# The first sixty microseconds of a hybrid backbone: modulation products in column tiles, and a gather of unit 0 beside the loads

## The chip, the core and the metric

The kernel runs on one core of a Trainium2 chip. The core has a TensorE for matrix products (PE in the profile; its weight loads are PEld), VectorE (DVE), ScalarE (ACT), GpSimd (POOL) and SyncE (SP), whose queue here issues nearly all transfers. TensorE's clock has two levels, 1.2 and 2.4 GHz; the profile shows the granted share of the higher one. The metric is the device time of one execution in microseconds. The bytes come from HBM into SBUF, products land in PSUM.

## What is computed

One layer of a diffusion backbone over 512 latent and 256 context tokens of width 1024. What matters here is its beginning:

```python
m_l = jax.nn.silu(c) @ w_ada[i] + b_ada[i]          # six vectors of 1024 for the latent
m_c = jax.nn.silu(c_ctx) @ w_ada[i] + b_ada[i]      # and for the context
u_l = modulate(x, sh1_l, sc1_l) @ w_in[i]           # modulate: layer_norm(x) * (1 + scale) + shift
u_c = modulate(xc, sh1_c, sc1_c) @ w_in[i]
mix_c, mix_l = token_mixer(u_c, u_l, ...)           # two scans in both directions, 8 heads
x = layer_norm(ALPHA * x + g1_l * (mix_l @ w_out[i]), ...)
y_l = peer(modulate(x, sh2_l, sc2_l), ...)          # product keys, 16384 experts of one neuron
x = layer_norm(ALPHA * x + g2_l * y_l, ...)
```

The first two of the six vectors (shift 1 and scale 1) are needed before any column of `u` can be computed. The gate of four of the heads is of rank 16: 32 columns of `u`, the gate rank, are multiplied by `w_gk2` later. All is in float32; the large products are made of three products of rounded parts (`mm3`: high by high, high by low, low by high).

## The kernel before

**Stages.** `Net.mixer` does the norm and modulation of all tokens (the pools `first` and `fps`), then six units of heads, each with `project` (its columns of `u`) and `scan`, then the output projection; `Peer` does the rest, about two thirds of the time. A loop in `mixer` calls `project`, `scan` and `mods_second` (m2, the other four vectors, one step at a time) by three running sums, and a list scheduler then places the instructions on the engines' queues by their dependences. Each queue runs in order.

**The beginning, by loops.** `mods_first` goes over four groups g of 512 columns of the first two vectors. A group has four loads `wada1` of 512 KB (two k of 128 rows each), eight products `pmr` that put the two conditions (latent, context) on 2 partitions by 512 columns and sum over k in PSUM, a copy `mrow`, four transposes `pm`, and two additions into `m1`. `first_norm` goes over six blocks b of 128 tokens (four latent, then two context): load `xin`, statistics, `xn`, eight transposes `pT`, two copies into `xt`. `modulate_first` makes, for each k of 128 channels and each of latent and context, the high part `hTh` on ScalarE and the low part `hTl` by two operations (`hT`, then `hTl`) on VectorE. `NN` says how many blocks are normed ahead of each group. Groups 0 and 1 give the k 0 to 3 their shifts and scales, and so on; k 0 to 5 are modulated behind group 2 and k 6, 7 behind group 3.

**Then**, one behind the other: `gate_rank` (32 products `pr`: 64 rows out of the columns `wr`, high and low), and in `project` of unit 0 the context values (`pt`, 24 products of 256 columns, a transposition), four blocks of 128 tokens by 256 columns of values and output gate (`pt`, 96 products), and the column products `pc` of `proj_c` for the two forget gates and the query. The value weights of unit 0, `w_tf`, are split into `wh` and `wl` by `token_slabs` ahead of that. PSUM tiles of the projections come from the pool `pj`, three buffers.

**Around it.** `scan_consts` (masks, lower bounds, six small loads) is called at the end of the beginning. `mods_second` first makes `silrow`, a row of 1024 conditions on all partitions (two halves, eight passes of ScalarE, four of VectorE), and then columns: each is a load of 256 KB and one operation of VectorE with a sum. It is stepped for the first time between groups 0 and 1. A transfer waits for the landing of the eighth ahead of it in the same queue, beside what its buffer waits for.

Of the kernel before, what the change touches and what calls it, by code (L numbers as in the profile page):

```python
# [8 lines left out]
F32 = mybir.dt.float32  # L9
F32R = mybir.dt.float32r  # L10
# [19 lines left out]


NN = (1, 3, 2, 0)


class Net:
# [112 lines left out]
    def mods_first(self, pers, pool, ps):  # L148

        nc, a = self.nc, self.a  # L150
        t1 = pool.tile([128, 8, 2], F32, name="cct1")
        t2 = pool.tile([128, 8, 2], F32, name="cct2")
        sil = pool.tile([128, 8, 2], F32, name="sil")
        self.log_sigmoid(sil, self.cc, t1, t2)
        nc.scalar.activation(sil, sil, AF.Exp)
        nc.vector.tensor_tensor(sil, sil, self.cc, op=OP.mult)
# [4 lines left out]
        for g in range(4):  # L161
            ws = [pool.tile([128, 2, 512], F32, name="wada1", bufs=8) for _ in range(4)]
            for i, w in enumerate(ws):
                nc.sync.dma_start(w, a["w_ada1"][g][:, i * 2:i * 2 + 2])
            p = ps.tile([2, 512], F32, name="pmr", bufs=2)
            for k in range(8):
                nc.tensor.matmul(p, sil[:, k, :], ws[k // 2][:, k % 2, :], start=k == 0, stop=k == 7)
            mrow = pool.tile([2, 512], F32, name="mrow", bufs=2)
            nc.vector.tensor_copy(mrow, p)
            pm = ps.tile([128, 4, 2], F32, name="pm", bufs=1)  # L170
            for m in range(4):
                nc.tensor.transpose(pm[:, m, :], mrow[:, m * 128:(m + 1) * 128], self.ident[0:2, 0:2])
# [3 lines left out]
            yield  # L176
# [89 lines left out]
    def first_norm(self, pool, ps, xt):  # L266

        nc, a = self.nc, self.a
        for b in (2, 3, 4, 5, 0, 1):
            x = pool.tile([128, D], F32, name="xin", bufs=2)  # L270
            nc.sync.dma_start(x, a["ctx"][b * 128:(b + 1) * 128] if b < 2 else a["x"][(b - 2) * 128:(b - 1) * 128])
            mu, rs = self.norm_stats(pool, x, "a")
            n = pool.tile([128, D], F32, name="xn", bufs=2)
            nc.vector.tensor_scalar(n, x, mu, rs, op0=OP.subtract, op1=OP.mult)
            for g in range(2):
                p = ps.tile([128, 4, 128], F32, name="pT")
                for i in range(4):
                    k = g * 4 + i
                    nc.tensor.transpose(p[:, i, :], n[:, k * 128:(k + 1) * 128], self.ident)
                nc.scalar.activation(xt[:, g * 4:g * 4 + 4, b * 128:(b + 1) * 128], p, AF.Copy)  # L280
            yield

    def modulate_first(self, pool, xt, ks):
# [461 lines left out]
    def mixer(self, es):  # L745
# [12 lines left out]
        with tc.tile_pool(name="first", bufs=1) as fp, tc.tile_pool(name="fps", bufs=2, space=PSUM) as fps:  # L758
# [11 lines left out]
            for g in range(4):  # L770
                for _ in range(NN[g]):
                    next(norm)
# [578 lines left out]
```

## Time and profile before

| | |
|---|---|
| median of three runs | 1774.92 us (1774.51 to 1775.79) |
| profiled execution | 1771.05 us, its span 1768.9 us |
| TensorE busy | 1711.5 us (97%), 10485 products |
| VectorE busy | 1448.7 us (82%) |
| ScalarE busy | 833.1 us (47%) |
| granted TensorE clock, mean | 0.988 |

A row of a timeline gives the start in us, the busy time of the group, engine, line, operation, tiles written and read, shapes (contraction rows by columns of the weights, then the moving operand), the count, and in brackets the idle time of the engine just before with what ended it. A matmul's record lasts longer than its share of the engine, since they are pipelined: the step from start to start is what one costs. In a row of groups, the figures behind the bar are busy us in sum, and mean ns of one.

### The profile page before, as it was taken

How to read it: one execution, taken by the hardware profiler on the slowest of the kernel's cores; microseconds unless marked ns; L12 is line 12 of the kernel's file. 1: busy time of each engine (PE TensorE's matmuls, PEld its weight loads, DVE VectorE, ACT ScalarE, POOL GpSimd, SP SyncE). 2: the span in 40 equal slices, each digit the busy share in tenths (PEclk: the TensorE clock that was granted, in tenths of full speed). 3: DMA queues.
4: the chain of work that ended last, by engine and by line, in shares of the span. 5: the costliest groups of instructions: out<-in, count | busy, mean ns of one | idle time of the engine just before them, and what ended most of it. 6: DMA issues, size and time to landing. Idle time of an engine off the chain costs nothing. (4 is left out here: it accounts for less than half of the span.)

```text
span 1768.9 us, 28164 instructions
## 1 busy us (share of the span) xinstructions
PE 1711.5 (97%) x10485; PEld 1484.2 (84%) x10485; DVE 1448.7 (82%) x2913; ACT 833.1 (47%) x1417; POOL 406.4 (23%) x285
## 2 busy tenths in 40 slices
PE   6999999999989999999999999999999999999997
PEld 2788887877778999999998899999999998888886
DVE  6669879877779999999996887787778786776768
ACT  5467676665233355776674333333333333333332
POOL 0000000000023102238522544344344442111000
PEclk9999999999989999999999999999999999999999
DMA  8523525415232247988999999989989989998862
GB/s 302 176 83 130 179 82 149 135 67 203 73 104 84 72 142 273 324 323 308 333 327 355 341 360 343 318 313 336 319 311 337 314 309 314 351 340 293 266 218 96
DMA packets 174811, 428.99 MB, mean 243 GB/s; under 512 B 14993, under 2 KB 78801, under 8 KB 170578
## 3 DMA queue, kind: packets, MB, share of 16 engines
q1 hardware_dynamic: 137234, 290.87, 48.5%
q0 software_dynamic: 36864, 134.23, 21.6%
q8 instruction: 82, 1.34, 0.3%
q10 hardware_dynamic: 576, 2.10, 0.3%
q14 instruction: 55, 0.45, 0.1%
HBM read 378.38 MB, written 48.76 MB: 241 GB/s over the span
## 5 line engine op out<-in xcount | busy, mean ns | idle before, releaser
L142 PE MATMUL pH<-hh,uh 128*128 128x384 f32 x1024 | 350.1, 342 | 1.0 <-ACT gels L1081 1.0
L144 PE MATMUL pH<-hh,ul 128*128 128x384 f32 x1024 | 347.6, 340 | 1.5 <-DVE ul L1068 1.5
L143 PE MATMUL pH<-hl,uh 128*128 128x384 f32 x1024 | 347.0, 339 | 0.0
L142 PE MATMUL y<-vh,ah 128*128 128x512 f32 x768 | 302.7, 395 | 4.1 <-ACT ah L1107 4.1
L144 PE MATMUL y<-vh,al 128*128 128x512 f32 x768 | 301.9, 395 | 0.4 <-DVE al L1108 0.4
L143 PE MATMUL y<-vl,ah 128*128 128x512 f32 x768 | 301.4, 392 | 0.0
L1068 DVE TENSOR_TENSOR vl<-vr,vh 128x1024 fp32r<-128x1024 f32 x128 | 156.7, 1224 | 154.9 <-ACT vh L1066 154.8
L1137 POOL DMA_INDIRECT erow<-in_u_dram,ix x128 | 188.8, 1475 | 371.7 <-DVE scr L1146 213.8
L1137 POOL DMA_INDIRECT erow<-in_v_dram,ix x128 | 184.2, 1439 | 327.9 <-DVE yg L1154 182.5
L1066 ACT ACTIVATE vh<-vr 128x1024 fp32r<-128x1024 f32 x128 | 135.1, 1056 | 200.4 <-issue 127.8
L1107 ACT ACTIVATE ah<-gel 128x384 fp32r<-128x384 f32 x128 | 66.8, 524 | 279.8 <-DVE gel L1104 278.0
L142 PEld LDWEIGHTS pH<-hh,uh 128*128 128x128 f32 x1024 | 192.4, 188 | 3.8 <-ACT gels L1081 1.4
L143 PEld LDWEIGHTS pH<-hl,uh 128*128 128x128 f32 x1024 | 192.7, 188 | 2.7
L144 PEld LDWEIGHTS pH<-hh,ul 128*128 128x128 f32 x1024 | 192.3, 188 | 2.5 <-DVE ul L1068 2.4
L1066 ACT ACTIVATE uh<-ur 128x1024 fp32r<-128x1024 f32 x128 | 135.0, 1055 | 116.3 <-PE pH L143 67.6
L144 PEld LDWEIGHTS y<-vh,al 128*128 128x128 f32 x768 | 144.7, 188 | 35.1 <-DVE al L1108 0.8
L142 PEld LDWEIGHTS y<-vh,ah 128*128 128x128 f32 x768 | 144.5, 188 | 34.9 <-ACT ah L1107 4.7
L143 PEld LDWEIGHTS y<-vl,ah 128*128 128x128 f32 x768 | 144.5, 188 | 30.7
L1068 DVE TENSOR_TENSOR ul<-ur,uh 128x1024 fp32r<-128x1024 f32 x128 | 155.7, 1217 | 15.7 <-PE pH L144 13.6
L1154 DVE SCALAR_TENSOR_TENSOR yg<-erow,act,yg 128x1024 f32<-128x1024 f32 x127 | 162.3, 1278 | 0.1
L1146 DVE SCALAR_TENSOR_TENSOR scr<-erow,h 128x1024 bf16<-128x1024 f32 x128 | 155.9, 1218 | 0.0
L142 PE MATMUL pc<-hTh,wh 128*128 128x512 f32 (+1 forms) x304 | 109.6, 361 | 0.4 <-ACT V L398 0.4
(358 smaller groups left out, 3055.8 us busy)
## 6 DMA issues: line engine op xcount, KB each, us to landing
ur<-in_uT_dram SPq DMA_DIRECT2D x128, 512.0 KB
vr<-in_v_dram SPq DMA_DIRECT2D x128, 512.0 KB
Gd<-stage SPq DMA_DIRECT2D x24, 1024.0 KB
Gn<-Gd SPq DMA_DIRECT2D x16, 1536.0 KB
wraw<-in_w_cf_dram SPq DMA_DIRECT2D x24, 512.0 KB
wada<-in_w_ada_dram SPq DMA_DIRECT2D x48, 256.0 KB
Hd<-gels SPq DMA_DIRECT2D x56, 192.0 KB
gel<-Hd SPq DMA_DIRECT2D x56, 192.0 KB
```

What stands on the lines that cost most here:

```text
L142: mm(out, lh, rh, start=start, stop=False)
L143: mm(out, lh, rl, start=False, stop=False)
L144: mm(out, ll, rh, start=False, stop=stop)
L1066: nc.scalar.activation(hi, raw, AF.Copy)
L1068: sub = eng.tensor_tensor(lo, raw, hi, op=OP.subtract)
L1107: nc.scalar.activation(ah, g, AF.Copy)
L1137: nc.gpsimd.indirect_dma_start(out=e, out_offset=None, in_=a[src], in_offset=bass.IndirectOffsetOnAxis(ap=self.ix[:, j:j + 1], axis=0))
L1146: nc.vector.scalar_tensor_tensor(scr, e, 1.0, h2, op0=OP.mult, op1=OP.mult, accum_out=dots[:, j:j + 1])
L1154: nc.vector.scalar_tensor_tensor(y, e, act[:, j:j + 1], y, op0=OP.mult, op1=OP.add)
```

## The change

Five things are done.

- `mods_first` gives `sil` 32 columns (two conditions, the rest zero) and puts product k on partitions 32 (k mod 4) and on, so that four products stand in four column tiles of 32; each tile sums two k. The sums of the four tiles are made by four products with `sel`, a selection of the partitions 0 and 1 of each 32, which take the place of the four transposes.
- `gate_rank` and the first part of `project` of unit 0 are gone; `begin` does, for one k after another, the three products of the context values, the two of the gate rank on context and two on latent, and the twelve of the values. It is stepped by two k, between the groups. The sums stay in PSUM over all eight k: all three buffers of `pj` (now the pool of the whole mixer) and one of `fps`.
- The loads: four blocks of x, then group 0, then the small ones of `scan_consts`, the context blocks, `wr`, the value weights, and groups 1 to 3. `first_norm` is one generator for each block, four buffers, and the norm is made in place.
- k 0 and 1 are modulated behind group 0 already, two k behind each group; latent and context of the first two k apart.
- `mods_second` is stepped for the first time in the loop over the units: its `silrow` and all its columns stand behind the beginning.

```diff
@@ mods_first
-        sil = pool.tile([128, 8, 2], F32, name="sil")
+        sil = pool.tile([128, 8, 32], F32, name="sil")
+        sc = sil[:, :, 0:2]
+        nc.vector.memset(sil, 0.0)
...
         for g in range(4):
+            yield
             ws = [pool.tile([128, 2, 512], F32, name="wada1", bufs=8) for _ in range(4)]
             for i, w in enumerate(ws):
                 nc.sync.dma_start(w, a["w_ada1"][g][:, i * 2:i * 2 + 2])
-            p = ps.tile([2, 512], F32, name="pmr", bufs=2)
+            yield
+            p = ps.tile([128, 512], F32, name="pmr", bufs=1)
             for k in range(8):
-                nc.tensor.matmul(p, sil[:, k, :], ws[k // 2][:, k % 2, :], start=k == 0, stop=k == 7)
-            mrow = pool.tile([2, 512], F32, name="mrow", bufs=2)
+                j = k % 4 * 32
+                nc.tensor.matmul(p[j:j + 32, :], sil[:, k, :], ws[k // 2][:, k % 2, :], start=k < 4, stop=k > 3)
+            mrow = pool.tile([128, 512], F32, name="mrow", bufs=2)
             nc.vector.tensor_copy(mrow, p)
             pm = ps.tile([128, 4, 2], F32, name="pm", bufs=1)
             for m in range(4):
-                nc.tensor.transpose(pm[:, m, :], mrow[:, m * 128:(m + 1) * 128], self.ident[0:2, 0:2])
+                nc.tensor.matmul(pm[:, m, :], mrow[:, m * 128:(m + 1) * 128], sel, start=m == 0, stop=m == 3)
@@ project
-            ws = self.ahead.pop(u, None) or self.token_slabs(u)
-            p = self.pj.tile([128, TC], F32, name="pt", tag="pj")
-            for k in range(8):
+            begun = self.ahead.pop(u, None)
+            ws = None if begun else self.token_slabs(u)
+            p = begun[0] if begun else self.pj.tile([128, TC], F32, name="pt", tag="pj")
+            for k in range(0 if begun else 8):
@@ begin
+        for k in range(8):
+            wh, wl = (t[:, k % 4, :] for t in slabs[k // 4])
...
+            for p, sl in ((pc, slice(0, TC)), (pl, slice(TC, TA))):
                 for i, h in enumerate((self.hTh, self.hTl)):
+                    nc.tensor.matmul(p, wr[:, k, :], h[:, k, sl], start=p is pl and k + i == 0,
+                                     stop=p is pl and k + i == 8)
...
+            for b in range(2, 6):
+                sl = slice(b * 128, (b + 1) * 128)
+                self.mm3(vg[b // 2 - 1][:, b % 2, :], self.hTh[:, k, sl], self.hTl[:, k, sl], wh, wl,
+                         k == 0 and b % 2 == 0, k == 7 and b % 2 == 1)
+            if k % 2:
+                yield
@@ mixer
-            norm, mods = self.first_norm(fp, fps, xt), self.mods_first(self.c, fp, fps)
-            seq = (0, 1, 4, 2, 5, 3)
-            for g in range(4):
-                for _ in range(NN[g]):
-                    next(norm)
-                if g == 1:
-                    next(m2)
-                if g == 2:
-                    self.ahead = {seq[0]: self.token_slabs(seq[0])}
-                next(mods)
-                if g > 1:
-                    self.modulate_first(fp, xt, range(0, 6) if g == 2 else range(6, 8))
-            self.scan_consts(self.mp, fp)
...
+            step(*norm[:4], mods, mods)
+            self.scan_consts(self.mp, fp)
+            step(norm[0], norm[1], norm[4], norm[5])
...
+            begin = self.begin(seq[0], fps, slabs, wr)
+            step(norm[2], norm[3], mods, mods)
+            self.modulate_first(fp, xt, range(0, 2), lat)
+            step(norm[4], norm[5])
+            self.modulate_first(fp, xt, range(0, 2), ctx)
+            for g in (1, 2, 3):
+                step(mods, begin, mods)
+                self.modulate_first(fp, xt, range(2 * g, 2 * g + 2), lat, ctx)
+            step(begin, begin)
...
-        self.gate_rank()
```

What the scheduler makes of it is seen in the queues. On TensorE, at the end of the third group and in the fourth, there stood before (`pmr` products of the groups' loads, `pm` transposes, then `pr`, the gate rank):

```order
L167 MATMUL pmr<-wada_428,sil 2x512 x2
L172 MATMUL pm<-ident,mrow 128x2 x4
L167 MATMUL pmr<-wada_429,sil 2x512 x2
L167 MATMUL pmr<-wada_430,sil 2x512 x2
L167 MATMUL pmr<-wada_431,sil 2x512 x2
L593 MATMUL pr<-hTh,wh 64x256
L593 MATMUL pr<-hTl,wh 64x256
```

and in the new order stand, from the first product of the fourth group on (`pt` are the gather's products, also those of `wrs`, the gate rank on context; `pr` is its gate rank on latent):

```order
L178 MATMUL pmr<-wada_529,sil 32x512 x2
L178 MATMUL pmr<-wada_530,sil 32x512 x2
L178 MATMUL pmr<-wada_531,sil 32x512 x2
L139 MATMUL pt<-hTh,wh 128x256
L140 MATMUL pt<-hTl,wh 128x256
L141 MATMUL pt<-hTh,wl 128x256
L610 MATMUL pt<-hTh,wrs 64x256
L610 MATMUL pt<-hTl,wrs 64x256
L178 MATMUL pmr<-wada_532,sil 32x512 x2
L610 MATMUL pr<-hTh,wrs 64x512
L610 MATMUL pr<-hTl,wrs 64x512
L139 MATMUL pt<-wh,hTh 128x256
```

The products of the fourth group have moved between those of the gather of k 4, and the gate rank has moved from behind all of them into the gather. On SyncE the queue began with one block, group 0 and two more blocks:

```order
L760 DMA cc<-in_ccol_dram 128x16
L762 DMA wr<-in_w_r_dram 128x256
L271 DMA xin<-in_x_dram 128x1024
L159 DMA b_140<-in_b1col_dram 128x16
L164 DMA wada_143<-in_w_ada_dram 128x1024
L164 DMA wada_144<-in_w_ada_dram 128x1024
L164 DMA wada_145<-in_w_ada_dram 128x1024
L164 DMA wada_146<-in_w_ada_dram 128x1024
L271 DMA xin<-in_x_dram 128x1024 x2
```

and now has (in brackets the semaphores waited for; `lbz`, `w` and `bgk` are small loads of `scan_consts`, a DMAHW semaphore counts the landing of an earlier transfer):

```order
L280 DMA xin<-in_x_dram 128x1024 x4
L167 DMA b_130<-in_b1col_dram 128x16
L173 DMA wada_133<-in_w_ada_dram 128x1024
...
L173 DMA wada_136<-in_w_ada_dram 128x1024 [waits DMAHW1_49]
L78 DMA lbz<-in_hg_lb_dram 128x8 [waits DMAHW2_49]
L100 DMA w_192<-in_w_gk_dram 16x256 [waits DMAHW3_49,DVE_49]
...
L103 DMA bgk<-in_b_gk_dram 128x4 [waits DMAHW7_49]
L280 DMA xin<-in_ctx_dram 128x1024 [waits DMAHW0_49,DVE_49,PE_49]
L280 DMA xin<-in_ctx_dram 128x1024 [waits DMAHW1_49,DVE_49,PE_49]
L798 DMA wr<-in_w_r_dram 128x256 [waits DMAHW2_49]
```

The small loads have moved from the end of the beginning to a place between group 0 and the context blocks. On VectorE, behind the last `hTl`, there stood before the columns of m2 (`wada,m2h`), ahead of the first gate operation of unit 0:

```order
L205 SCALAR_TENSOR_TENSOR wada_1347,m2h<-wada_1347,silrow 128x512
L301 TENSOR_TENSOR wl<-wraw,wh 128x1024
L205 SCALAR_TENSOR_TENSOR wada_1350,m2h<-wada_1350,silrow 128x512
L301 TENSOR_TENSOR wl<-wraw,wh 128x1024
L205 SCALAR_TENSOR_TENSOR wada_1353,m2h<-wada_1353,silrow 128x512
L209 TENSOR_TENSOR m_242<-m2h 128x8
L115 SCALAR_TENSOR_TENSOR gs_717<-G,gs_716 128x512
L210 TENSOR_TENSOR m_242<-m_242,b2col 128x8
L329 TENSOR_TENSOR G<-G,gs_717 128x512
L205 SCALAR_TENSOR_TENSOR wada_1625,m2h<-wada_1625,silrow 128x512
```

and now, from the second half of `silrow` on, the columns stand between those of the gate (`gs`, `Z`, `LF`, up to the scan `BP`):

```order
L309 TENSOR_TENSOR wl<-wraw,wh 128x1024
L215 SCALAR_TENSOR_TENSOR wada_1100,m2h<-wada_1100,silrow 128x512
L112 SCALAR_TENSOR_TENSOR gs_757<-Z,gs_756 128x768
L215 SCALAR_TENSOR_TENSOR wada_1245,m2h<-wada_1245,silrow 128x512
L387 SCALAR_TENSOR_TENSOR Z<-gs_757,lbl_185,Z 128x768
L215 SCALAR_TENSOR_TENSOR wada_1248,m2h<-wada_1248,silrow 128x512
L391 TENSOR_SCALAR gs_757<-gs_757,lbl_185,lbA 128x768
L215 SCALAR_TENSOR_TENSOR wada_1251,m2h<-wada_1251,silrow 128x512
L392 TENSOR_TENSOR LF<-gs_757,gs_756 128x768
L215 SCALAR_TENSOR_TENSOR wada_1254,m2h<-wada_1254,silrow 128x512
L437 SCALAR_TENSOR_TENSOR BP<-rmask,LF 128x768
```

The weighted columns have moved behind the gate's first operations and the row `silrow` has come with them.

## Rows read from the trace of the kernel before

**Rows 1.** Windows: busy us (instructions) of PE, PEld, DVE, ACT, POOL; clock, DMA, GB/s.

```profile
20.00:40.00 20.00, 14.01 (x53) 4.92 (x53) 13.40 (x24) 11.96 (x23) 0.00 (x0) 0.91 0.90 337
...
60.00:80.00 20.00, 19.53 (x142) 18.37 (x142) 11.88 (x28) 6.00 (x12) 0.00 (x0) 1.00 0.69 202
80.00:100.00 20.00, 19.00 (x114) 16.68 (x113) 13.32 (x26) 13.14 (x19) 0.00 (x0) 1.00 0.48 147
```

**Rows 2.** Timeline of TensorE, 10 to 74 us.

```profile
10.96 6.17 PE L167 MATMUL pmr<-wada,sil 128*2 128x512 f32 x14
17.06 1.10 PE L279 MATMUL pT<-ident,xn 128*128 128x128 f32 x8
...
53.15 0.40 PE L172 MATMUL pm<-ident,mrow 2*128 2x2 f32 x4
...
57.55 0.39 PE L593 MATMUL pr<-hTh,wh 128*64 128x512 f32 x1
57.78 0.40 PE L593 MATMUL pr<-hTl,wh 128*64 128x512 f32 x1
...
61.83 0.36 PE L142 MATMUL pt<-wh,hTh 128*128 128x256 f32 x1
...
73.43 0.40 PE L142 MATMUL pc<-hTh,wh 128*128 128x512 f32 x1
```

**Rows 3.** Timeline of VectorE: its first statistics of a block.

```profile
5.36 1.29 DVE L122 BATCH_NORM_STATS2 sta<-xin 128x6 f32<-128x512 f32 x2 [0.75 <-DMA xin<-in_x_dram]
```

**Rows 4.** VectorE by groups, shapes apart, the first 75 us.

```profile
L205 DVE SCALAR_TENSOR_TENSOR wada<-wada,silrow 128x512 f32<-128x512 f32 x13 | 8.8, 690 | 7.3 <-DMA wada<-in_w_ada_dram 7.2
L122 DVE BATCH_NORM_STATS2 sta<-xin 128x6 f32<-128x512 f32 x12 | 7.8, 681 | 2.3 <-DMA xin<-in_x_dram 2.2
L291 DVE TENSOR_TENSOR hTl<-hT,hTh 128x512 fp32r<-128x512 f32 x8 | 5.4, 673 | 0.0
L274 DVE TENSOR_SCALAR xn<-xin,mva,rsa 128x1024 f32<-128x1024 f32 x6 | 4.8, 806 | 0.6 <-ACT rsa L131 0.6
L290 DVE TENSOR_SCALAR hT<-xt,m 128x512 f32<-128x512 f32 x8 | 4.3, 541 | 0.9 <-ACT xt L280 0.9
L301 DVE TENSOR_TENSOR wl<-wraw,wh 128x1024 fp32r<-128x1024 f32 x3 | 3.7, 1218 | 2.4 <-ACT wh L300 2.4
...
L128 DVE BATCH_NORM_AGGREGATE mva<-sta 128x2 f32<-128x12 f32 x6 | 1.2, 199 | 0.1
```

**Rows 5.** Timeline of TensorE: products on two column tiles, and on four tiles.

```profile
129.43 0.69 PE L514 MATMUL psc<-q,Z 128*64 128x64 f32 x16
129.94 0.40 PE L514 MATMUL psc<-arg 128*64 128x64 f32 x6
130.30 0.49 PE L478 MATMUL pkv<-V,KT 128*128 128x128 f32 x2
...
258.12 0.69 PE L514 MATMUL psc<-arg 64*64 64x64 f32 x32
258.74 0.71 PE L255 MATMUL prow<-ident,m 128*128 128x128 f32 x4
```

**Rows 6.** Windows: the same columns, two stretches of the beginning.

```profile
28.30:35.00 6.70, 3.38 (x17) 1.43 (x16) 6.36 (x13) 5.62 (x11) 0.00 (x0) 0.98 0.84 278
35.00:38.40 3.40, 3.10 (x4) 0.47 (x5) 1.85 (x3) 1.64 (x4) 0.00 (x0) 0.54 1.02 408
```

**Rows 7.** Timelines of VectorE, ScalarE and TensorE, 85 to 105 us.

```profile
85.96 0.69 DVE L205 SCALAR_TENSOR_TENSOR wada<-wada,silrow 128x512 f32<-128x512 f32 x1 [3.47 <-DMA wada<-in_w_ada_dram]
...
90.13 0.95 DVE L115 SCALAR_TENSOR_TENSOR gs<-Z,gs 128x768 f32<-128x768 f32 x1
...
95.28 1.76 DVE L428 TENSOR_TENSOR_SCAN BP<-rmask,LF 128x768 f32<-128x768 bf16 x1
...
85.98 0.94 ACT L114 ACTIVATE gs<-gs,one 128x768 f32<-128x768 f32 x1
...
103.99 0.69 PE L355 MATMUL pt<-ident,Z 128*128 128x128 f32 x2 [2.93 <-ACT Z L352]
```

More of the change, by code (lines that the diff above doesn't have):

```diff
@@ L29 @@
 NB = 2
-NN = (1, 3, 2, 0)
 class Net:
@@ L263, in mod_row, with first_norm, modulate_first @@
         return r
-    def first_norm(self, pool, ps, xt):
+    def first_norm(self, pool, ps, xt, b):
         nc, a = self.nc, self.a
[L269 to L283, printed above, removed]
+        x = pool.tile([128, D], F32, name="xin", bufs=4)
+        nc.sync.dma_start(x, a["ctx"][b * 128:(b + 1) * 128] if b < 2 else a["x"][(b - 2) * 128:(b - 1) * 128])
+        yield
+        mu, rs = self.norm_stats(pool, x, "a")
+        nc.vector.tensor_scalar(x, x, mu, rs, op0=OP.subtract, op1=OP.mult)
+        for g in range(2):
+            p = ps.tile([128, 4, 128], F32, name="pT")
+            for i in range(4):
+                k = g * 4 + i
+                nc.tensor.transpose(p[:, i, :], x[:, k * 128:(k + 1) * 128], self.ident)
+            nc.scalar.activation(xt[:, g * 4:g * 4 + 4, b * 128:(b + 1) * 128], p, AF.Copy)
+    def modulate_first(self, pool, xt, ks, *parts):
         nc = self.nc
         for k in ks:
-            for i, j, s in ((TC, TA, 0), (0, TC, 1)):
+            for i, j, s in parts:
                 sc, sh = self.m1[:, 8 + k, s:s + 1], self.m1[:, k, s:s + 1]
@@ L358, in project @@
             for b in (2, 4):
-                p = self.pj.tile([128, 2, 256], F32, name="pt", tag="pj")
-                for i in range(2):
+                p = begun[b // 2] if begun else self.pj.tile([128, 2, 256], F32, name="pt", tag="pj")
+                for i in range(0 if begun else 2):
                     sl = slice((b + i) * 128, (b + i + 1) * 128)
@@ L756, in mixer @@
         self.mp = pool(el, "mix")
+        self.pj = pool(ep, "pj", space=PSUM, bufs=3, side="right")
         m2 = self.mods_second(self.c, m2p)
@@ L760, in mixer @@
             nc.sync.dma_start(self.cc, self.a["ccol"])
+            xt = fp.tile([128, 8, TA], F32, name="xt")
+            self.hTh, self.hTl = (hp.tile([128, 8, TA], F32R, name=n) for n in ("hTh", "hTl"))
+            self.rT = self.mp.tile([64, TA], F32, name="rT")
+            seq = (0, 1, 4, 2, 5, 3)
+            mods = self.mods_first(self.c, fp, fps)
+            norm = [self.first_norm(fp, fps, xt, b) for b in (2, 3, 4, 5, 0, 1)]
+            step = lambda *gens: [next(g, None) for g in gens]
@@ L761, in mixer @@
+            lat, ctx = (TC, TA, 0), (0, TC, 1)
+            step(*norm[:4], mods, mods)
+            self.scan_consts(self.mp, fp)
+            step(norm[0], norm[1], norm[4], norm[5])
             raw = fp.tile([128, 8, 32], F32, name="wr")
             nc.sync.dma_start(raw, self.a["w_r"])
[L763 to L765 removed]
@@ L780, in mixer @@
-            self.scan_consts(self.mp, fp)
+            slabs = self.token_slabs(seq[0])
+            wr = fp.tile([128, 8, 64], F32R, name="wrs")
+            nc.scalar.activation(wr[:, :, 0:32], raw, AF.Copy)
+            nc.vector.tensor_tensor(wr[:, :, 32:64], raw, wr[:, :, 0:32], op=OP.subtract)
+            self.ahead = {}
+            begin = self.begin(seq[0], fps, slabs, wr)
+            step(norm[2], norm[3], mods, mods)
+            self.modulate_first(fp, xt, range(0, 2), lat)
+            step(norm[4], norm[5])
```

45 lines of the change are left out of this document (24 added, 21 removed).

## The prediction

> **What bounds the kernel now.** The windows come first [rows 1]. Read TensorE's column beside VectorE's: from 60 us on TensorE is busy for 19.5 of 20 us, and the same holds for most of the 1768.9 us span (97% on the page). In the first 40 us it waits. So the change, which touches only the first 60 us and the order of a few loads behind them, is worth what it moves one point: the first column product of unit 0, `pc`, which starts at 73.43 us [rows 2]. Everything behind it is a chain of TensorE work whose waits are relative to it; no clock time stands in the way later.
>
> The TensorE timeline [rows 2] is read next. Products of the modulation vector (`pmr`) come 0.43 us apart (14 records in 6.17 us less the tail of the last); the built order has 7 products there, so an fp32 product is two records, and the 32 products are 64 x 0.43 = 27.5 us, stretched by waits for loads to about 52 us. Only then come, one behind the other: the last transposes (53.15), the gate rank (up to 58.0), the context values (up to 61) and 96 value products from 61.83 to 73.43, that is 11.60 / 96 = 0.121 us each for 256 columns. For 512 columns it is 57.78 - 57.55 = 0.23 us.
>
> **The change part by part.** The sum goes by engine, in three stretches, up to the start of `pc`.
>
> *First stretch: VectorE, to about 35 us.* It starts when the first x block lands, 5.4 us in the trace [rows 3]; now one small load fewer is ahead, so 4.9. Four blocks are normed in a row: 4 x (2 x 0.64 + 0.20 + 0.80) = 9.1 us (the means of [rows 4] less the 0.04 us by which neighbours overlap). Between them stand 12 mask operations and some 9 small ones, at 0.2 us as the aggregation: 4.2. That is 18.3 us, and the loads keep ahead. Then group 0 closes: the last block's transposes (8 in 1.0 us [rows 2]), three products left over abreast 0.9, copy 0.65, the fold that replaces the transposes 0.8 (8 records at the 0.1 of row 53.15), two additions 0.2: 21.8. Latent modulation of two k is 2 x (0.50 + 0.60) = 2.2 and five small operations 0.9: 24.9. The two context blocks 4.6, two halves of `wl` 2.4, the gate weights 0.4, modulation of the first k on context about 1.0, and some 1.5 of waits for ScalarE and transposes: about 35. The loads don't bound it: 12.7 MB at the 337 GB/s of 20 to 40 us [rows 1] end near 41 us, and group 3 isn't wanted before 50.
>
> *Second stretch: TensorE, from 33.5 us.* One gather is per k 3 + 2 + 12 products of 256 columns and 2 of 512: 17 x 0.121 + 2 x 0.23 = 2.5 us. Eight are 20.1; 0.9 of it (gate rank of the first two k) is done earlier: 19.2. Of the modulation products 20 are left. They are now 32 columns wide, in four column tiles. The trace has no such shape, but two neighbours [rows 5]: 16 records of 64 columns in two column tiles take 0.51 us, 32 ns each, and 32 records in four tiles of 64x64 take 0.62 us, 19 ns each; one after the other they would take 53 ns (half of the 107 ns that a 128-column record takes in [rows 2]: 1.10 us for eight, less the 0.24 us tail). So four tiles run nearly abreast, and I take 0.86 us for up to four products whose loads are in. Ends: serial 20 x 0.86 = 17.2 us, four abreast without pairs 20 / 4 x 0.86 = 4.3. By the built order the 20 stand in seven pieces (2, 2, then 4, 2, 2, then 6, 2 of which the 6 take two turns): 8 x 0.9 = 7.2. Changing between tiled and whole products costs about 0.1 to 0.2 us: 6 records at 32 ns would end at 130.13, the next product starts at 130.30 [rows 5]. Seven pieces, twice: 1.4. Three folds 2.4. Sum 19.2 + 7.2 + 1.4 + 2.4 = 30.2, so the gathers end at 63.7. Before, those same 27.5 us of products lay under the loads; now most of the gather lies behind them, and what pays is that the products shrink.
>
> TensorE: Matmul & The Clock Gate (the Trainium skill), section Part 3: Packing small matmuls, says that matmuls start in strict program order even when they run abreast on different tiles. With two records per product on the same tile that would let only two tiles run at a time, and the 7.2 would be 11.6. The 19 ns of the four-tile row speak against it, so it is a rival below and not the forecast.
>
> *Third stretch: ScalarE.* All three PSUM buffers of the projections are held by the gather, so `pc` waits until two are emptied. ScalarE has then just split two slabs and begun the conditioning row: `pc` starts about 0.8 us behind the gather, 64.5.
>
> *Clock.* TensorE is idle from about 21 to 27 us in the new order. Before, 6.7 us in which TensorE was busy for 3.4 were followed by 3.4 us at a mean granted clock of 0.54, the 1.2 GHz level for nearly all of it [rows 6], where every product takes twice as long. I add 1.5 us (bounds 0 and 3.4): 66.0. Against 73.43 that is **-7.4 us**.
>
> *Behind that point.* The conditioning row (2.7 us on VectorE) and 11 of the weighted columns at 0.69 us, 10.3 us together, were done on VectorE ahead of `pc` and now stand behind it, between unit 0's gate operations. Who waits is TensorE: it stood 2.93 us for unit 1's first transposes, at 103.99, 30.6 us behind `pc` [rows 7]. The chain to there runs over the first gate operation of VectorE (90.13) and its scan (95.28, 21.9 behind `pc`). ScalarE had the gate's input ready at 85.98 + 0.94 = 86.9, 13.5 behind `pc`; VectorE came 3.2 us later, since it stood in a column that waited for its load (3.47 us before 85.96 alone). In the built order four columns now stand between gate and scan where one stood, 3 x 0.69 = 2.1 us more, but the gate operation itself no longer has a column with a late load ahead of it. So the scan comes 13.5 + 5.15 + 2.1 = 20.8 us behind `pc`, against 21.9, and VectorE has 8.1 and 6.7 us idle in 60 to 80 and 80 to 100 us to take the columns before [rows 1]. I cost the push at 0, with ends -1 (that difference) and +10 (none of that idle time can be used, because a column there waits for its load).
>
> *At nothing:* the new zero fill, two operations that make the selection, and the iota lie ahead of the first x block; the in-place norm changes no count; six small loads stand among the big ones, each behind the landing of one ahead, and delay the context blocks to about 20 us, where VectorE wants the first at 25.
>
> The profiled execution took 1771.05 us, 2.2 around its span of 1768.9; the median of the three runs is 1774.92, 3.9 above it. I take the 7 us off the median: **1768 us**, own range 1764 to 1772 (clock and drain).
>
> **The rivals.**
> *Only two tiles abreast.* The 20 products cost 0.86 for the first and 0.43 for each further one of a piece: 11.6 in place of 7.2, the group 0 chain 0.5 later: gain 2.5, 1772.4. For: two passes share a tile. Against: 19 ns in four tiles.
>
> *One after the other.* 17.2 in place of 7.2 and 1.7 in group 0: 1775 - 7 + 11.7 = 1779.6. That is slower, with the same operations. Against: both tiled rows of [rows 5].
>
> *VectorE becomes the bound behind `pc`* (the slower side). Place: unit 1's transposes. Price: up to the 10 us of above, and a longer stand of TensorE can bring another stretch at half clock, 3 us [rows 6]. From 7 us of delay on it eats the gain; at the full price 1768 + 10 = 1778, 1781 with the clock. For: the conditioning row takes ScalarE too, eight passes of it, and a column may wait for its load at the new place as well. Against: the idle VectorE of [rows 1].
>
> *More than forecast.* No half clock at the start, and no stretch at half clock behind the stand at 104 us, of the size of the one in [rows 6]: 1.5 + 3 more: about 1763.
>
> *The gather doesn't lie beside the loads.* It hardly does: I have it behind the loads already, so this costs nothing more.
>
> **How the numbers follow.** Forecast 0.58, more 0.10, two abreast 0.12, serial 0.05, VectorE the bound 0.15. A measurement of this kernel can tell about 0.2%, 3.5 us, from no change: faster is under 1771.4, slower over 1778.5. Faster: nearly all of the forecast, all of the better case, a third of two abreast, 0.70. Same: the rest of two abreast, and the half of the VectorE case that costs 4 to 10 us, 0.20. Slower: serial and the rest of it, 0.10. The range goes from 1762 to 1777.
>
> **What would show it.** `pc` at about 66 us, 64 to 69. Four `pmr` records starting within a fraction of 0.43 us. Gathers without gaps on TensorE from about 35 to 64 us, VectorE without gaps before. Last group's loads in by 42. First scan 20 to 23 us behind `pc`, and TensorE's stand for unit 1's transposes of about 3 us. From 130 us on every stage earlier by the same 7 us. I am wrong if `pc` is later than 70, if `pmr` records come 0.43 us apart, or if the lead at `pc` is gone by 130 us.

## The result, and the profile of the changed kernel

Over 20 runs each the changed kernel took 1768.04 us (median) and the kernel before 1774.73; the ratio is 0.9948, 95% interval 0.9928 to 0.9967. That is 6 to 13 us less. The profiled execution took 1758.76 us.

The page of the changed kernel, its span and the busy time of the engines (instructions):

```profile
span 1756.6 us, 28197 instructions
...
PE 1699.8 (97%) x10501; PEld 1486.9 (85%) x10501; DVE 1447.2 (82%) x2917; ACT 833.2 (47%) x1417; POOL 406.7 (23%) x286
```

TensorE is busy for 11.7 us less than the 1711.5 of before and idle for about as long. Where the time went is read at the beginning. The windows that answer to [rows 1], and below them two of 10 us (columns as there):

```profile
20.00:40.00 20.00, 13.41 (x77) 8.54 (x78) 13.91 (x35) 9.61 (x20) 0.00 (x0) 0.74 0.92 344
60.00:80.00 20.00, 19.75 (x119) 17.42 (x118) 13.05 (x22) 16.61 (x30) 0.00 (x0) 1.00 0.59 176
80.00:100.00 20.00, 17.57 (x112) 16.18 (x111) 19.41 (x38) 13.92 (x24) 0.00 (x0) 0.91 0.56 168
```

```profile
20.00:30.00 10.00, 3.94 (x16) 2.79 (x16) 8.10 (x22) 5.77 (x12) 0.00 (x0) 0.56 1.00 395
30.00:40.00 10.00, 9.47 (x62) 5.74 (x62) 5.81 (x13) 3.84 (x10) 0.00 (x0) 0.93 0.84 293
```

From 20 to 30 us TensorE works for 3.9 us at a mean granted clock of 0.56, so mostly at the 1.2 GHz level; from about 31.4 us on the clock is full, up to the waits behind 90 us. VectorE is busy for 8.1 of the 10 us from 20 to 30. The timeline of TensorE, which answers to [rows 2] (`pmr` the products of the modulation vector, `pm` their fold, `pt` and `pr` the gather, `pc` the first column product of unit 0):

```profile
12.63 1.90 PE L178 MATMUL pmr<-wada,sil 128*32 128x512 f32 x8
...
15.49 1.04 PE L178 MATMUL pmr<-wada,sil 128*32 128x512 f32 x2
...
19.38 1.05 PE L183 MATMUL pm<-sel,mrow 128*128 128x2 f32 x8 [0.83 <-DVE mrow L180]
26.49 1.97 PE L288 MATMUL pT<-ident,xin 128*128 128x128 f32 x8 [6.06 <-DVE xin L283]
...
34.40 0.39 PE L139 MATMUL pt<-hTh,wh 128*128 128x256 f32 x1 [0.24 <-ACT hTh L296]
...
40.77 1.06 PE L178 MATMUL pmr<-wada,sil 128*32 128x512 f32 x8
41.76 0.39 PE L139 MATMUL pt<-hTh,wh 128*128 128x256 f32 x1
...
42.44 1.05 PE L178 MATMUL pmr<-wada,sil 128*32 128x512 f32 x4
43.42 0.34 PE L610 MATMUL pt<-hTl,wrs 128*64 128x256 f32 x1
...
50.13 1.91 PE L178 MATMUL pmr<-wada,sil 128*32 128x512 f32 x12
51.97 0.39 PE L139 MATMUL pt<-hTh,wh 128*128 128x256 f32 x1
...
54.72 0.95 PE L183 MATMUL pm<-sel,mrow 128*128 128x2 f32 x8
55.53 0.36 PE L140 MATMUL pt<-wl,hTh 128*128 128x256 f32 x1
...
64.68 0.50 PE L139 MATMUL pc<-hTh,wh 128*128 128x512 f32 x1 [0.25 <-ACT G L376]
```

Read three things. First, eight `pmr` records (four products) take 1.06 us and four records (two products) 1.05; the next instruction starts 0.99 and 0.98 us after them. Before, a record alone cost 0.43 us [rows 2]. Second, the rows from 34.40 on have no idle time in brackets up to `pc`. Third, `pc` starts at 64.68 us in place of 73.43: 8.75 us earlier.

On VectorE the modulation of the first two k on the context ends at 35.29 us, and the first scan of unit 0 starts 19.4 us behind `pc` (21.85 before [rows 7]); TensorE's waits around the transposes of unit 1 are shorter than the 2.93 us of before [rows 7] and the 0.79 and 0.20 ahead of it. First three rows of VectorE (the first is read further down, where the forecast is compared), then the waits of TensorE from 60 to 135 us (in total, times, longest), now and, last, two of before:

```profile
18.63 0.69 DVE L180 COPY mrow<-pmr 128x512 f32<-128x512 f32 x1 [2.38 <-PE pmr L178]
...
34.38 0.91 DVE L299 TENSOR_TENSOR hTl<-hT,hTh 128x256 fp32r<-128x256 f32 x2 [0.24 <-ACT hTh L296]
...
84.10 1.75 DVE L437 TENSOR_TENSOR_SCAN BP<-rmask,LF 128x768 f32<-128x768 bf16 x1
```

```profile
PE pkt L481 <- ACT K L468: 1.7, 1, 1.7
PE pt L364 <- ACT Z L361: 0.8, 1, 0.8
```

```profile
PE pt L144 <- DVE wl L301: 0.8, 1, 0.8
PE pkt L472 <- ACT K L456: 0.2, 1, 0.2
```

By the first `pkv`, at 106.4 us, the lead is 11.9 us: the 8.75, 1.5 of shorter waits, and 1.7 since the stretch at 1.2 GHz behind those waits was 3.4 us and not 6.8 long. At the end of the two profiles it is 12.3 us. The medians differ by 6.7 us here and by 12.4 us in the second sample (again, below): the times of either kernel spread by 15 to 22 us, and they go with the mean granted clock (last section).

### The profile page after: what moved, and what is told of

Its sections match the earlier page's. It is cut to its first block, busy times and chain, and to the rows that moved or that the text cites. A ratio compares the mean times of both kernels' runs of the same rounds, so it can differ in the third digit from the quotient of the medians.

```text
span 1756.6 us, 28197 instructions
## 1 busy us (share of the span) xinstructions
PE 1699.8 (97%) x10501; PEld 1486.9 (85%) x10501; DVE 1447.2 (82%) x2917; ACT 833.2 (47%) x1417; POOL 406.7 (23%) x286
```

## The experiments

All kernels are compared with the kernel before on the same chip. The second column is the start of `pc` in the profile, the point on which the prediction rests; profiles of the same kernel agree there within 0.1 us (64.68 and 64.58), while medians of 6 to 20 runs move by some 3 us.

| kernel | first `pc`, us | median, us (before beside it) | ratio, 95% interval |
|---|---|---|---|
| before | 73.43 | | |
| changed (first result) | 64.68 | 1768.04 (1774.73) | 0.9948 (0.9928 to 0.9967) |
| again | 64.58 | 1764.43 (1776.85) | 0.9947 (0.9919 to 0.9974) |
| onetile | 76.76 | 1778.02 (1776.85) | 1.0014 (0.9994 to 1.0035) |
| nogather | 78.15 | 1774.86 (1776.85) | 0.9991 (0.9970 to 1.0013) |
| tilesonly | 80.53 | 1784.30 (1776.85) | 1.0035 (1.0015 to 1.0056) |
| warm | 65.66 | 1764.23 (1776.43) | 0.9937 (0.9919 to 0.9955) |
| nogwarm | 75.30 | 1778.18 (1776.43) | 1.0019 (0.9998 to 1.0040) |
| silrow | 69.54 | 1772.10 (1776.43) | 0.9968 (0.9950 to 0.9987) |
| silstore | 68.60 | 1774.34 (1777.56) | 0.9987 (0.9967 to 1.0006) |
| silone | 65.79 | 1766.31 (1775.72) | 0.9949 (0.9930 to 0.9969) |
| befnom2 | 72.78 | 1775.57 (1777.56) | 0.9993 (0.9975 to 1.0010) |
| latfirst | 66.83 | 1769.12 (1776.43) | 0.9960 (0.9942 to 0.9978) |
| latforce | 58.64 | 1763.02 (1777.56) | 0.9920 (0.9894 to 0.9947) |

Through the 13 kernels, a line of the median over the start of `pc` has a slope of about 0.93 us per us: what the beginning gains arrives at the end. Single kernels lie up to 5 us off it, so the time of a single one cannot tell differences of a few us at `pc`.

**again**: the changed kernel itself.

> The changed kernel once more, beside the three below. The time differs between executions by 10 us and more while the first column product of unit 0 is expected at 64.7 us in each, so that the difference lies behind it. If the whole spread is the granted clock of TensorE behind the beginning, then time and mean clock of the runs fall on one line: 0.01 of the mean clock is about 17 us, as in the 20 runs of the result (0.976 at 1780.99, 0.989 at 1758.66). Rival: the beginning itself varies between runs; then the first column product moves by several us between profiles.

The start of `pc` stayed within 0.1 us, the time went from 1759.4 to 1774.8 us over 11 runs. Over the 31 runs of the changed kernel, time and mean granted clock correlate with -0.90, and 0.01 of the clock is 18.6 us. The spread goes with the clock behind the beginning, as the theory had it, and not with the beginning.

**onetile**: the tiles taken back, gather and loads kept.

```diff
-                nc.tensor.matmul(p[j:j + 32, :], sil[:, k, :], ws[k // 2][:, k % 2, :], start=k < 4, stop=k > 3)
+                nc.tensor.matmul(p[0:32, :], sil[:, k, :], ws[k // 2][:, k % 2, :], start=k == 0, stop=k == 7)
...
```

> All eight products of a group stand on one column tile of 32; the fold takes the sum from 32 partitions; everything else as changed. Theory (four tiles run abreast, 0.89 us for four products in place of 3.4): the products come 0.43 us per record again, 20 x 0.86 = 17.2 us in place of 7.2 behind the first context block, and group 0 closes 2 to 3 us later: first column product at 75 to 78 us, time 10 to 12 us above the changed kernel. Rival (the tiles bring nothing, the reordering does it): first column product at 64 to 67, time within 3 us of the changed kernel.

TensorE's timeline, one group in a row:

```profile
44.95 7.05 PE L177 MATMUL pmr<-wada,sil 128*32 128x512 f32 x16
...
76.76 0.50 PE L139 MATMUL pc<-hTh,wh 128*128 128x512 f32 x1
```

16 records in 7.05 us, so 0.43 us each and 3.5 us for four products where four tiles take 0.98. `pc` came 12.1 us later than with the tiles: the theory held. The time is 13.6 us above that of again, where 10 to 12 was expected. With the gather but without the tiles `pc` comes 3.3 us later than in the kernel before; the time cannot be told from it (0.9994 to 1.0035).

**nogather**: tiles and loads kept, `gate_rank` and the first part of `project` of unit 0 as before.

```diff
-            begun = self.ahead.pop(u, None)
-            ws = None if begun else self.token_slabs(u)
+            begun = None
+            ws = self.ahead.pop(u, None) or self.token_slabs(u)
...
-                step(mods, begin, mods)
+                step(mods, mods)
...
+        self.gate_rank()
```

> The tiles and the new order of loads stay; the gate rank, the context values and the values of unit 0 are made as before, one behind the other with all k of a block in a row. Theory (the gather matters since TensorE has work while VectorE modulates): 96 products of 0.121 us, 11.6 us, stand behind the last modulation, so the first column product comes at about 71 us (68 to 72), time 5 to 7 us above the changed kernel. Rival (TensorE is full from 34 us on in either order, so only the sum of its work counts): at 64 to 66 us, within 2 us of the changed kernel.

Windows of the beginning and the start of `pc`:

```profile
30.00:40.00 10.00, 7.92 (x35) 3.85 (x31) 4.36 (x8) 2.63 (x7) 0.00 (x0) 0.61 0.67 232
60.00:70.00 10.00, 9.12 (x45) 8.10 (x45) 4.82 (x9) 7.23 (x14) 0.14 (x2) 0.57 0.18 54
```

```profile
78.15 0.40 PE L139 MATMUL pc<-hTh,wh 128*128 128x512 f32 x1
```

78.15: even later than my 71, and later than before. Without the gather TensorE has little to do, the clock is at the 1.2 GHz level for long stretches (0.61 and 0.57 in these windows, 0.93 and 1.00 in the changed kernel), and the 96 value products start under it. Theory and rival both missed: `pc` is 13.5 us later than with the gather. Behind `pc` this kernel got back 3.6 us (its first `pkv` came 41.3 us behind `pc`, 44.9 before), and its time cannot be told from that of the kernel before.

**tilesonly**: the kernel before with tiles and fold, nothing else.

```diff
-                nc.tensor.matmul(p, sil[:, k, :], ws[k // 2][:, k % 2, :], start=k == 0, stop=k == 7)
+                j = k % 4 * 32
+                nc.tensor.matmul(p[j:j + 32, :], sil[:, k, :], ws[k // 2][:, k % 2, :], start=k < 4, stop=k > 3)
...
```

> The kernel before with the column tiles and the fold alone; loads, norms, gate rank and values as before. Theory: the products shrink from 27.5 to about 8 us, but six k are modulated behind group 2 (about 2 us of VectorE each, 12 us) and the 11.6 us of values stand behind the last modulation, so only 2 to 4 us are gained: first column product at 69 to 72, time 2 to 4 us under the kernel before. Rival (the tiles are the whole gain): at 64 to 66, 8 us under it.

First the two windows of the kernel before, then those of tilesonly, then two blocks of transposes on TensorE, and `pc`:

```profile
30.00:40.00 10.00, 6.38 (x25) 2.36 (x25) 6.94 (x13) 5.56 (x11) 0.00 (x0) 0.83 1.01 378
40.00:50.00 10.00, 10.00 (x31) 2.33 (x30) 9.22 (x24) 5.54 (x10) 0.00 (x0) 1.00 0.81 285
```

```profile
30.00:40.00 10.00, 4.35 (x26) 2.79 (x23) 6.45 (x13) 6.67 (x14) 0.00 (x0) 0.68 0.93 338
40.00:50.00 10.00, 8.95 (x36) 4.30 (x36) 6.49 (x13) 4.17 (x8) 0.00 (x0) 0.64 0.77 262
```

```profile
36.88 1.97 PE L288 MATMUL pT<-ident,xn 128*128 128x128 f32 x8 [3.67 <-DVE xn L283]
41.05 1.97 PE L288 MATMUL pT<-ident,xn 128*128 128x128 f32 x8 [2.20 <-DVE xn L283]
...
80.53 0.40 PE L142 MATMUL pc<-hTh,wh 128*128 128x512 f32 x1
```

`pc` comes 7.1 us later than before, and the time is 0.15 to 0.56% longer: the opposite of what both theories had. The products did shrink. But the 27.5 us of them had kept TensorE busy [rows 2]; now it waits 3.67 and 2.20 us for VectorE's norms, the clock falls (0.68 and 0.64 in windows where before it was 0.83 and 1.00), eight transposes take 1.97 us in place of 1.09, and the list scheduler stands the last groups' products between those of the gate rank, six times as a pair alone, so that the values start at 67.25 and not at 61.83, and at the 1.2 GHz level. How the 7.1 us divide between the clock, the pairs and the order was not separated.

**warm and nogwarm**: how much of that is the clock? Both add products whose sums nobody uses, warm to the changed kernel and nogwarm to nogather; the diff is that of warm, and nogwarm has three behind each of the other groups as well.

```diff
+            if g == 0:
+                for m in range(6):
+                    nc.tensor.matmul(p, self.ident, mrow, start=True, stop=True)
```

> The changed kernel with six more products of 128 columns by 512 behind the fold of group 0, 0.86 us each, 5.2 us; their sums are used by nothing. They fill TensorE's stand from 20.4 to 26.5 us. Theory: the granted clock stays at 1.0 there (it was the 1.2 GHz level from 21.2 to 31.4), the transposes of the context blocks and the products up to 31.4 take half as long, and since they mostly wait for VectorE and ScalarE this is worth 0 to 1.5 us: first column product at 63.2 to 64.7, time 0 to 2 us under the changed kernel. Rival (the half clock there costs its full size, 5 us of work at half speed, or a later half clock takes its place): first column product under 62.5, or not earlier and a new stretch at 1.2 GHz before 65 us.

> The kernel without the gather once more, with filling products whose sums nothing uses, 0.86 us each: six behind the fold of group 0, three behind each of the others. Without them its first column product came at 78.2 us, with 17.1 us at the 1.2 GHz level from 20.8 and 10.2 us from 58.3. Theory (the loss against the 71 us that was expected is the clock): with the clock at 1.0 throughout it comes at 70 to 73.5 us. Rival (the order alone costs it, the clock nothing): at 77 us or later.

The windows of warm:

```profile
20.00:30.00 10.00, 8.35 (x33) 3.62 (x32) 8.38 (x23) 5.88 (x12) 0.00 (x0) 1.00 1.01 393
30.00:40.00 10.00, 8.15 (x45) 5.14 (x46) 4.69 (x10) 2.75 (x6) 0.00 (x0) 0.83 0.79 285
```

With the clock at 1.00 from 20 to 30 us the theory's gain did not come: the norm of the second context block on VectorE, for which TensorE waits in that stretch at either clock, started at 30.99 us in warm and at 31.22 in the changed kernel, and warm had been 0.34 us ahead before the filling. So the full clock brought nothing up to that point. Behind it came 3.4 us at the lower level, from 32.3 on, and `pc` stood at 65.66, 1.0 us later: the second rival (a later stretch takes its place) held. A beginning with neither stretch was not seen.

In nogather the filling brought `pc` from 78.15 to 75.30; theory and rival both missed. The filling itself takes TensorE's time, and 3.4 us at the lower level were left, so the clock is at least 2.9 us of its loss; how the rest divides between the clock and the order was not settled.

**silrow, silstore, silone**: the push of the second vectors behind the beginning, taken back.

```diff
             for g in (1, 2, 3):
+                if g == 1:
+                    next(m2)
                 step(mods, begin, mods)
```

> The changed kernel with the first step of the second vectors (the row silrow: 8 passes of ScalarE, 4 of VectorE, two loads) called between groups 0 and 1 as before; only one weighted column stays ahead of the first column product. Theory (the push behind it costs nothing, VectorE has the idle time): first column product at 64.2 to 65.7, TensorE's stands at 88 to 95 us within 1 us of the 2.4 us they have, time within 2 us of the changed kernel. Rival (the push costs): the stands go to under 1 us and the time is 2 to 4 us less.

`pc` at 69.54, 4.9 us later than in the changed kernel. I had missed it: I had looked behind `pc` only. There the theory held: TensorE's waits behind `pc` are again 2.4 us (1.6 and 0.8), so the push costs nothing behind it. SyncE's waits named a suspect, the store of `silrow`, which stands ahead of group 3's last load (wait in total, times, longest):

```profile
SPq L208 <- DVE silrow L207: 15.7, 1, 15.7
```

silstore issues that store one step later and leaves everything else.

```diff
-        nc.sync.dma_start(self.sild, sr[0:1].rearrange("p h k -> p (h k)"))
         yield True
+        nc.sync.dma_start(self.sild, sr[0:1].rearrange("p h k -> p (h k)"))
```

> The run with the early silrow once more, its first column product at 69.5 us, with one thing altered: the small store of silrow to HBM, which stood in SyncE's queue ahead of the last load of group 3 and waited there 15.7 us for silrow, is issued one step later, behind the loads of the beginning. The operations of silrow on VectorE and ScalarE stay where they were. Theory (the blocked queue is the cause): the last load of group 3 is issued before 36 us in place of 50.2, the fold of group 3 comes at 54 to 56 in place of 60.3 and the first column product at 64.2 to 66, time within 2 us of the changed kernel. Rival (the 12 operations in the middle of the chain of folds are the cause): at 68 to 70.

68.60, in the range of the rival: without the waiting store `pc` comes 0.9 us earlier, so the store is not the main cause. (In silrow the window from 60 to 70 us also has a granted clock of 0.83, in silstore 1.00.) What is left in the timeline of silstore is this, compared with the pieces of the changed kernel above:

```profile
46.34 1.05 PE L178 MATMUL pmr<-wada,sil 128*32 128x512 f32 x4
...
57.73 1.05 PE L178 MATMUL pmr<-wada,sil 128*32 128x512 f32 x4
...
64.12 0.45 PE L610 MATMUL pr<-hTl,wrs 128*64 128x512 f32 x1 [1.18 <-DVE hTl L299]
...
68.60 0.50 PE L139 MATMUL pc<-hTh,wh 128*128 128x512 f32 x1
```

Groups 2 and 3 stand in eight pieces of one pair each, two of which are shown. A pair takes as long as four products, so from the first gather product on there are nine turns of the four tiles in place of seven, 2.0 us more. And at 64.12 TensorE waits 1.18 us for the modulation behind the last fold, a wait that the changed kernel does not have. silone is silstore with one load of 2 MB for each of groups 1 to 3, so that the eight products of a group are ready, and stand, together.

```diff
-            ws = [pool.tile([128, 2, 512], F32, name="wada1", bufs=8) for _ in range(4)]
+            ws = pool.tile([128, 8, 512], F32, name="wada1", bufs=2)
+            if g:
+                nc.sync.dma_start(ws, a["w_ada1"][g])
...
```

> The run with the early silrow and the late store once more (first column product at 68.6 us), with one thing altered: each of groups 1 to 3 comes by one load of 2 MB in place of four, so that its eight products stand in a row on TensorE's queue. There the products of groups 2 and 3 stood in eight pieces of one pair each, and a pair alone took 0.98 us, as long as four products together. Theory (the pieces are what the early silrow cost): groups 1 to 3 take 6 turns of the four tiles in place of 11, so 5 x 0.98 = 4.9 us less; first column product at 63.5 to 66 us, time 3 to 5 us under that run. Rival (the operations of silrow, or the later fold of group 3, cost it, not the pieces): at 67.5 or later, time within 1.5 us of that run.

```profile
46.93 1.92 PE L180 MATMUL pmr<-wada,sil 128*32 128x512 f32 x16
...
54.81 1.92 PE L180 MATMUL pmr<-wada,sil 128*32 128x512 f32 x16
...
65.79 0.50 PE L139 MATMUL pc<-hTh,wh 128*128 128x512 f32 x1
```

Eight products in 1.92 us, and `pc` at 65.79: 2.8 us earlier than silstore, in the range of the theory, with `silrow` called at the same place. Group 1 came later and at the 1.2 GHz level (eight products in 3.64 us from 35.85). The rival (the operations of `silrow` or the later fold cost it: 67.5 or later) did not come, so the pieces are a large part of what held silstore back. That the loads of `silrow`, which stand between those of the groups, make the pieces is read from the queue and was not tested alone. And no run has the 2 MB loads without the early `silrow`, though the changed kernel has pieces to lose as well, so its share of the 2.8 us is not known.

**befnom2**: the push alone, on the kernel before (`next(m2)` between the groups left out).

> The kernel before with one thing altered: the first step of the second vectors is not called between groups 0 and 1 but in the loop over the units, as in the changed kernel. In the kernel before its store waited 5.7 us at the head of SyncE's queue, to 27.75 us, ahead of the second context block, half of the value weights and the eight loads of groups 2 and 3. Theory (that wait is a share of the gain): these come about 6 us earlier, group 2's products start at 29 to 32 in place of 35.3, the first column product comes at 68 to 71 in place of 73.4, time 2 to 5 us under the kernel before. Rival (the serial products and VectorE bound that stretch anyway): at 72.5 or later, within 1.5 us.

Its window from 30 to 40 us, its products of group 2 and `pc`:

```profile
30.00:40.00 10.00, 7.71 (x20) 2.33 (x21) 4.38 (x9) 3.93 (x7) 0.00 (x0) 0.66 1.01 390
```

```profile
33.76 5.88 PE L167 MATMUL pmr<-wada,sil 128*2 128x512 f32 x8 [1.29 <-DMA wada<-in_w_ada_dram]
...
72.78 0.40 PE L142 MATMUL pc<-hTh,wh 128*128 128x512 f32 x1
```

The rival held: 0.65 us, and the store that waited 5.7 us in SyncE's queue gave the kernel before no more than that. Group 2's products did start earlier, at 33.76 in place of 35.30, but at a lower clock (0.66 from 30 to 40 us, 0.83 before), so some of what the earlier loads gave may have gone to the clock.

**latfirst and latforce**: a further step. In latfirst the value weights are loaded ahead of the context blocks and the latent part of k 0 and 1 is gathered ahead of them, in TensorE's wait of 6.06 us before 26.49.

```diff
             step(norm[2], norm[3], mods, mods)
             self.modulate_first(fp, xt, range(0, 2), lat)
-            step(norm[4], norm[5])
+            step(begin, norm[4], norm[5])
             self.modulate_first(fp, xt, range(0, 2), ctx)
+            step(begin)
...
```

> A further step: the value weights are loaded ahead of the context blocks, the gather of the latent part of k 0 and 1 (24 value products, 4 of the gate rank, 3.8 us) is called ahead of the context blocks, and the small loads behind group 2's. Theory: TensorE's stand from 20.4 to 34 us takes 3.8 us of gather and the fold of group 1 as well, so that the first column product comes at 56 to 61 us, time 4 to 8 us under the changed kernel. Rival (VectorE is the bound of the whole beginning, and it has the same operations; or the context part comes too late): at 63 to 66 us, within 2 us of it.

66.83, and no gain: later than either theory had it. The timeline shows why: the last group's products in a row, the wait behind their fold, and `pc`:

```profile
55.74 1.06 PE L178 MATMUL pmr<-wada,sil 128*32 128x512 f32 x8
...
59.84 0.69 PE L616 MATMUL pr<-hTh,wrs 128*64 128x512 f32 x1 [1.17 <-ACT hTh L296]
...
66.83 0.50 PE L139 MATMUL pc<-hTh,wh 128*128 128x512 f32 x1
```

The loads of group 3 were issued by 34.3 us, but its products stand at 55.74 behind gather work, and TensorE then waits for the fold and the modulation (and the window from 60 to 70 us has a granted clock of 0.86). latforce lets no part of the gather of k 2 to 5 start ahead of the next group's products, and alters two things more, as its expectation says.

```diff
+                    with tc.issue_after(self.last[g + 1]):
+                        step(begin)
...
```

> The run with the latent part first once more (first column product at 66.8 us), with three things altered: the products of group 1 are called ahead of the context blocks, those of groups 2 and 3 are made to stand ahead of the gather of k 2, 3 and of k 4, 5 on TensorE's queue, and the small loads come behind group 3. There the loads of group 3 were in by about 36 us and its last products stood at 55.7, behind gather work that could have waited, so that TensorE waited for the fold afterwards. Theory (the order of products on TensorE lost what the earlier start gained): the fold of group 3 comes at 42 to 50 us, no wait of more than 0.5 us for a fold behind 40, first column product at 57 to 62, time 3 to 7 us under the changed kernel. Rival (VectorE's chain of norms and modulations bounds it): at 63 to 66, within 2 us of the changed kernel.

```profile
45.19 1.92 PE L179 MATMUL pmr<-wada,sil 128*32 128x512 f32 x16
...
48.20 0.95 PE L185 MATMUL pm<-sel,mrow 128*128 128x2 f32 x8
...
58.64 0.50 PE L139 MATMUL pc<-hTh,wh 128*128 128x512 f32 x1
```

The fold comes at 48.20 and nothing waits for it. `pc` stands at 58.64, 6.0 us earlier than in the changed kernel, with the same operations on VectorE, so VectorE was not what held latfirst. Three things were altered together, so what each gave is not shown. The time is 0.53 to 1.06% under the kernel before. At `pc` it beats the changed kernel; in time that is not shown, since the intervals overlap and only six runs were taken.

## Why the prediction was right, and where it was not

The forecast was 1768, -7.4 us, with `pc` at 66.0. It held: 1768.04, and `pc` at 64.68. That the median fits to 0.04 us is luck: the second sample has 1764.43, 12.4 us under the kernel before. In the profiles the lead is 8.75 us at `pc` and about 12 at the first `pkv` and at the end, where the forecast had the same 7.4 throughout.

*First stretch.* Forecast: VectorE full to about 35 us, gathers from 33.5. Measured: 35.29 and 34.40. VectorE was not full: four waits from 16 to 35 us take 6.2 us (2.38 for group 0's products, at 18.63, then 1.07, 1.36 and 1.38), where the sum had 4.2 (1.5, and 2.7 for group 0's transposes, products and fold). Its operations were costed too long by about as much, so the end came out right by two errors that cancel.

*Second stretch.* Forecast 30.2 us: gather 19.2, 20 products of the groups 7.2 with 1.4 for the changes between tiled and whole, folds 2.4. Measured from 33.10 (the first piece of these 20) to 64.05: 30.95. The pieces took 7.7 us with the changes in them (six of 0.98 and one of two turns, 1.84; the forecast had 8.6), the folds 0.81 each, and the rest, 20.8, is the gather and its short waits. So the pieces were sized 0.9 us too large and the gather 1.6 too small. The rival of two tiles abreast falls with the rows: four products take what two take. The serial one falls with onetile, which also gives its price: 12.1 us, where the rival had 11.7.

*Clock.* This is the term that was mis-sized: 1.5 us. The three measured stretches (33.10, 30.95 and 0.63) add up to 64.68, and the forecast's sum without the term was 64.5. I had seen that TensorE would be idle and slow from 21 us, and charged for it, though in the same stretch I had VectorE as the bound. warm shows no gain from the full clock there, though a later slow stretch came with it.

*Third stretch.* 0.8 us forecast, 0.63 measured (64.05 to 64.68).

*Behind that point.* The push at no cost, the scan 20.8 us behind `pc`: measured 19.4, and the waits of TensorE fell from 3.9 to 2.4 us, 0.5 us beyond the end of -1 that I gave. Two of the signs that I named did not come: the scan 20 to 23 us behind `pc`, and a stand of about 3 us for unit 1's transposes (0.8 us there, and 1.7 us before it). The rival of VectorE as the bound (1778 to 1781) did not come. The rival "more than forecast" came in half: the stretch at 1.2 GHz behind the waits was 3.4 us shorter in the one profile and absent in the other.

*What the forecast did not know.* It says that what pays is that the products shrink, and costs the push and the order of the gather at nothing or nearly. Here its mechanism fails, though its sum does not: without the gather `pc` is 13.5 us later, and with `silrow` back in its place 4.9. The sum came out right because it took its pieces from the built order, in which all parts are together. The runs show the parts apart: tiles alone +7.1 us at `pc`, gather and loads without tiles +3.3, tiles and loads without gather +4.7, all without the push -3.9, the push alone -0.65; together -8.75. The parts do not add up to that. As I read it, the tiles empty TensorE and the gather fills it; the push keeps the groups' loads, and so their products, together. In my expectations for tilesonly and nogather I costed the parts at the full clock, and missed by 9 and 7 us.

What stays open: how much of the loss of nogather and tilesonly is the scheduler's order. nogwarm puts the clock's share in one of them at 2.9 us or more.

## What to carry to other kernels

A product that is made cheaper on the bound engine pays only as far as other work is ready to take its place; if none is, the engine waits, its clock can fall to the lower level, and the kernel can get slower (tilesonly). Small products packed side by side pay by turns and not by products: see to it that the operands of a whole turn are there together, by the size and order of the loads, and look at the built order for pieces that are alone. Where a scheduler sets the order, cost a change on the whole built order, since its parts do not add up.

## What the runs showed of the hardware

- *Four column tiles run abreast for float32.* Four products of 32 columns by 512, two records each, take 0.98 us up to the next instruction, a pair alone takes the same, and one after the other they take 3.5 us. In the trace the first records of the four start 6 to 7 ns apart, and the second records together 0.45 us later. The Trainium skill, TensorE: Matmul & The Clock Gate, Part 3: Packing small matmuls, says that matmuls start in strict program order; if the two records of a product followed each other in that order, only two tiles could run. The trace does not agree with that reading.
- *The time of a kernel spreads with the mean granted clock.* For the changed kernel it went from 0.976 at 1780.99 us to 0.989 at 1758.66, and 0.01 is 18.6 us (31 runs, correlation -0.90); for the kernel before 17.6 us (100 runs, -0.74). At 0.986 the two lines stand at 1764.5 and 1776.2 us, 11.7 us apart, close to the 12.3 of the two profiles; the medians, at whatever clocks their runs had, are 6.7 us apart in the first result. A kernel also makes its own clock, so this comparison is no cleaner measure of the change. The same page, Part 1: The HAM clock gate, says of the slow stretch at the start of a kernel that it varies from run to run; here the slow stretches in the middle do so too: behind the waits of unit 1 it was 3.4 us long in one profile of the changed kernel and absent in the other.
- *A wait ahead of dense work can cost twice.* In tilesonly two waits of 3.67 and 2.20 us were followed by transposes at 1.97 us in place of 1.09.
